# State-space loop: each projection's products in a row, conditioning columns and evictions moved, the last input matrices ahead of the state products

## The chip, the cores and the metric

One core of a Trainium2 chip runs one kernel. The metric is the device time of the whole kernel in microseconds, as the median of runs; smaller is better. The engines are TensorE (PE, with its weight loads PEld), VectorE (DVE), ScalarE (ACT), GpSimd (POOL) and SyncE (SP); the last two mostly issue transfers here. Each runs its own instructions strictly in the order in which the program has them, and waits for others by semaphores.

## The reference

Two residual layers over a sequence of 512 tokens of width 1024 in float32. The first layer mixes tokens with a state-space model (64 groups of 16 channels, 64 complex states each), the second with forgetting attention; each is followed by a gated convolutional feed-forward block, and each sub-layer is modulated by columns that a conditioning vector gives. Only the state-space layer is touched:

```python
def adaln_params(c, w, b):
    mod = jax.nn.silu(c) @ w + b
    shift, scale, gate = jnp.split(mod, 3, axis=-1)
...
def s5_mixer(h, w_in, lam_re, lam_im, log_dt, b_re, b_im, c_re, c_im, d_skip, w_glu, w_out):
    u = h @ w_in                                  # projection
    ug = u.reshape(Bsz, S, S5_GROUPS, S5_GROUP)
    ...                                           # lb: state decay, bb: input matrix
    # state[l] = lb * state[l-1] + bb @ u[l];  y[l] = Re(c @ state[l])
    y = y + d_skip.astype(f32) * u.astype(f32)
    y = jax.nn.gelu(y)
    y = y * jax.nn.sigmoid(y @ w_glu.astype(f32))
    return (y @ w_out.astype(f32)).astype(h.dtype)
```

## The kernel before

The method `s5` does this layer with channels in 8 tiles (`KT`) of 128, eight groups of channels to a tile. Time is cut in 64 blocks (`B`) of 8 steps (`L`). Inside a block the answer to the inputs is a product with a small Toeplitz matrix; from block to block the states go by a scan on VectorE. The loop over `m` in `range(KT - 2)` does tile `m`, and prepares tiles `m + 1` and `m + 2` beside it; tiles 6 and 7 follow behind the loop, in the tail. Within `tc.manual_schedule` every engine gets its instructions in the order in which the code issues them: the order of the Python lines is the order of the work, and nothing else sets it. A tile of a pool that has no free room waits until the last reader of that room is done.

The steps of iteration `m`, with the lines under which the profile has them:

- `s5_blocks(m)`, "blocks", L1089: 16 products on TensorE, block inputs into states; they need `u` and `w1` of tile m.
- `inputs(m + 1)`, "input matrices", L1029: 8 products out of `x` (a sum made by VectorE, `s5_states_in`, L991 and L1001) and of the planes `s5_both` (ScalarE, L1016). Their four results go through four PSUM rooms of the pool `aux`, which ScalarE empties into `w1` (L1034) and `kt` (L1038).
- `s5_scan(m)`: seven instructions on VectorE, L1105 to L1120, whose result is `ua`. They need the factors `cf` (ScalarE, L1074) and the rotations `rot` (made ahead on VectorE, L968 to L970, and copied on ScalarE, L977 and L983).
- `s5_kernel(m + 1)` adds to `kt` (VectorE, L1046) and stores it to DRAM (`s_z`, SP, L1049); `s5_toeplitz(m + 1)` reads it back spread out as `tw` (SP, L1056); `s5_masked(m)` makes `t` of an earlier `tw` (ScalarE, L1065, eight instructions).
- `project(m + 2)`, "projection", L1259: 8 products of 128x512, split in `steps[:4]`, `steps[4:5]`, `steps[5:6]`, `steps[6:7]` and `steps[7:]`; `done()` evicts them to `uf` (ScalarE, L1264) and stores it (`s_ud`, SP, L1265), and `read_u(m + 2)` reads it back turned (SP, L1269).
- `s5_from_inputs(m)`, "input products", L1130: 8 products of `t` and `u` into two PSUM rooms; `s5_from_states(m)`, "state products", L1141: 16 products of `ua` and `w2` (`s5_states_out`, VectorE, also L991 and L1001; two rooms) into the same two.
- `s5_gelu(m)`, "yg", L1154: two evictions on ScalarE, then a store (`s_yd`, SP, L1155); `s5_read_y` reads it back as `h` (SP, L1158).
- `next(ada)` and `next(ada2)`, "columns", L226: each call multiplies the conditioning vector with a part of the modulation matrix; two calls stand in most iterations. The last call of `ada` (in iteration 1) also evicts the sum (`ada_rows`, ScalarE, L235), and one more, in iteration 2, turns it into columns (L165, L170, L178). Their matrices are loaded by POOL (L194) into rooms that they share with the weights.
- `part_hi` (ScalarE, L1285) and `part_lo` (VectorE, L1288) split y in two parts; `head_raw` loads the first weights of `w_glu` (POOL, L194), `head_hi` and `head_lo` split them (L1295, L1299), and `glu_head` (TensorE, L1304) begins the next product in the tail.

The two arrangements of the order that matter are these: half of the projection stands ahead of the input products and the rest is scattered behind them, and yg is issued between the state products and the last projection.

Of the kernel before, what the change touches and what calls it, by code (L numbers as in the profile page):

```python
# [20 lines left out]
KT = D // P  # L21
# [58 lines left out]
class Trunk:  # L80
# [71 lines left out]
    def done(self):  # L152
        while self.bg:
            assert next(self.bg.pop(0), None) is None
# [663 lines left out]
class S5(Trunk):  # L818
# [341 lines left out]
    def s5(self, i, nxt):  # L1160
# [7 lines left out]
        with ExitStack() as stack:  # L1168
# [82 lines left out]
            us, ws, w2s, tws, cfs, kts, dds, yps = ({} for _ in range(8))  # L1251

            def run(steps):
                for f in steps:
                    f()
# [19 lines left out]
            def inputs(m, beside=None):  # L1275
                ws[m], kts[m] = self.s5_inputs(m, x_in.pop(m), beside)
# [30 lines left out]
            with tc.manual_schedule(engines={ENG.PE, ENG.Activation, ENG.DVE, ENG.SP, ENG.Pool}):  # L1307
# [35 lines left out]
                for m in range(KT - 2):  # L1343
                    if m + 3 < KT:
                        load_w(m + 3)
                    load_d(m + 2)
                    ps = self.s5_blocks(ws[m], us[m])
                    inputs(m + 1)
                    st = self.s5_scan(rot[:, :, m % 2 * 4:m % 2 * 4 + 4], ps, cfs.pop(m))
                    self.s5_kernel(m + 1, kts.pop(m + 1), dds.pop(m + 1))  # L1350
                    next(turns)
                    t = self.s5_masked(tws.pop(m))
                    tws[m + 1] = self.s5_toeplitz(m + 1)
                    if m:
                        self.s5_read_y(m - 1)
                    steps, done = project(m + 2)
                    run(steps[:4])
                    yp, outs = self.s5_from_inputs(us[m], t)
                    run(outs[:8] + steps[4:5])
                    if m == 2:  # L1360
                        next(ada)
                    run(steps[5:6] + outs[8:])
                    self.s5_planes_of(m + 2)
                    x_in[m + 2] = self.s5_states_in(m + 2)
                    if m == 2:
                        yhi = self.act.tile([P, KT, S], F32R, name="y_hi", tag="a_lo")
                        aux = self.aux.tile([KT, P], F32, name="aux")
                        nc.tensor.transpose(aux, self.sc, self.ident)
                        rows = self.tmp.tile([KT, P], F32, name="nm_h", bufs=4)
                        nc.scalar.activation(rows, aux, AF.Copy)  # L1370
                        nc.sync.dma_start(self.scd, rows)
                    if m >= 2:
                        part_hi(m - 2)
                    if m == KT - 3:
                        run(steps[6:])
                        done()
                        read_u(m + 2)
                    w2s[m + 1] = self.s5_states_out(m + 1)
                    if m % 2:
                        rot = next(turns)  # L1380
                    cfs[m + 1] = self.s5_factors(m + 1)
                    outs = self.s5_from_states(yp, w2s.pop(m), st)
                    if m < KT - 3:
                        run(outs[:16] + steps[6:7] + outs[16:])
                        self.s5_gelu(m, yp)
                        if m == 1:
                            next(ada)
                            next(ada2)
                        else:
                            next((ada, ada2)[m > 1])  # L1390
                        run(steps[7:])
                        done()
                        read_u(m + 2)
                        next((ada, ada2)[m > 1])
                    else:
                        run(outs)
                        self.s5_gelu(m, yp)
                        next(ada2)
                        inputs(KT - 1)
                        t = self.s5_masked(tws.pop(KT - 2))  # L1400
                        next(ada2)
                    us.pop(m)
                    ws.pop(m)
                    if m == KT - 4:
                        head_raw(0)
                        head_raw(1)
                    if m == KT - 3:
                        head_raw(2)
                        head_raw(3)
                    if m % 2 and m + 3 < KT:  # L1410
                        turns = self.s5_rotations(m + 3)
                        next(turns)
                m = KT - 2
                ps, ps2 = (self.s5_blocks(ws[n], us[n]) for n in (m, m + 1))
                self.s5_kernel(m + 1, kts.pop(m + 1), dds.pop(m + 1))
                self.s5_read_y(m - 1)
                tws[m + 1] = self.s5_toeplitz(m + 1)
                w2s[m + 1] = self.s5_states_out(m + 1)
                yp, outs = self.s5_from_inputs(us[m], t)
                run(outs)  # L1420
                ylo = self.act.tile([P, KT, S], F32R, name="y_lo", tag="a_hi")
                for n in range(HEAD):
                    gps[n] = self.mm.tile([P, S], F32, name="mmp")
                head_hi(0)
                part_hi(m - 2)
                head_hi(1)
                for n in range(2):
                    for k in range(5):
                        glu_head(k, 0, (n,))
# [433 lines left out]
```

## Time and profile before

| | us |
|---|---|
| median of 3 runs | 1218.91 (1216.08 to 1222.62) |
| the profiled execution | 1213.14 |
| its span in the profile | 1211.3 |
| the loop, from the input products of iteration 0 to the blocks of the tail | 64.09 to 162.38 |
| the tail, to the last state products' end | 162.38 to 180.9 |

The profile is of one execution, so its numbers add up to 1213.14 and not to the median. A row of the order of time has its start and length in us, the engine, the line, what is written and read, and how many instructions; in brackets stands idle time of the engine before it, and what ended that. A product of float32 operands is two records of TensorE. In the chain that ended last, TensorE's lines have 35% and VectorE's 5% of the span; the rest of the chain is not followed by the profile.

### The profile page before, as it was taken

The numbers are of one execution on the slowest core, as the hardware profiler recorded it, in microseconds if no ns is written. First come the engines' busy times: TensorE is split into PE (matmuls) and PEld (weight loads), VectorE is DVE, ScalarE is ACT, GpSimd is POOL, SyncE is SP. The second block draws the span as 40 slices with busy tenths as digits, with TensorE's granted clock in tenths as the row PEclk, the third lists the DMA queues.
The fourth block names the chain that finished last, engine by engine and source line by source line (L and its number), as shares of the span: only waits on it lengthen the run. The fifth ranks groups of instructions, "written<-read, shape, count | busy, mean of one in ns | idle before, by whom it ended". The sixth has DMA issues, their size and how long they took to land. (4 is left out here: it accounts for less than half of the span.)

```text
span 1211.3 us, 20642 instructions
## 1 busy us (share of the span) xinstructions
PE 1179.9 (97%) x7925; PEld 1018.7 (84%) x7925; DVE 1010.1 (83%) x1868; ACT 615.1 (51%) x1179; POOL 113.5 (9%) x194
## 2 busy tenths in 40 slices
PE   7989999999999999999999999999999999999997
PEld 2556678898889889999999788878989999999987
DVE  8968896879989999998797678876899888888865
ACT  3545553435545445555443566664366555545543
POOL 0212111100000000000000344430000000000000
PEclk9889999999999999999999999999999999999999
DMA  9658758732354555433445443432223332323331
GB/s 365 261 176 287 232 189 280 269 126 70 95 193 148 175 170 173 149 113 101 126 142 193 164 165 128 149 126 88 71 70 97 122 121 89 103 93 110 109 101 70
DMA packets 71825, 181.99 MB, mean 150 GB/s; under 512 B 23103, under 2 KB 24479, under 8 KB 70703
## 3 DMA queue, kind: packets, MB, share of 16 engines
q1 hardware_dynamic: 58767, 137.94, 34.7%
q0 software_dynamic: 11632, 41.95, 10.0%
q8 instruction: 62, 1.02, 0.3%
q10 hardware_dynamic: 1328, 0.79, 0.2%
q14 instruction: 36, 0.29, 0.1%
HBM read 173.73 MB, written 6.92 MB: 149 GB/s over the span
## 5 line engine op out<-in xcount | busy, mean ns | idle before, releaser
L301 DVE TENSOR_TENSOR w_lo<-raw,w_hi 128x1024 fp32r<-128x1024 f32 (+4 forms) x173 | 180.4, 1047 | 24.8 <-ACT w_hi L300 24.3
L300 ACT ACTIVATE w_hi<-raw 128x1024 fp32r<-128x1024 f32 (+4 forms) x173 | 153.9, 899 | 92.5 <-PE mmp L317 42.2
L317 PE MATMUL mmp<-ghi,w_lo 128*128 128x512 f32 (+1 forms) x412 | 147.6, 358 | 1.3 <-DVE w_lo L301 1.1
L317 PE MATMUL mmp<-ghi,w_hi 128*128 128x512 f32 (+1 forms) x412 | 147.8, 359 | 0.0
L317 PE MATMUL mmp<-glo,w_hi 128*128 128x512 f32 (+1 forms) x412 | 147.5, 358 | 0.0
L317 PE MATMUL mmp<-a_hi,w_hi 128*128 128x512 f32 (+1 forms) x320 | 116.7, 368 | 1.5 <-ACT a_hi L469 1.5
L586 PE MATMUL mmp<-w_hi 128*128 128x256 f32 x420 | 116.5, 277 | 1.5 <-ACT nm_h L593 1.0
L586 PE MATMUL mmp<-w_lo,w_hi 128*128 128x256 f32 x420 | 116.1, 276 | 0.0
L586 PE MATMUL mmp<-w_hi,w_lo 128*128 128x256 f32 x420 | 115.9, 277 | 0.0
L317 PE MATMUL mmp<-a_hi,w_lo 128*128 128x512 f32 (+1 forms) x320 | 114.4, 358 | 0.0
L317 PE MATMUL mmp<-a_lo,w_hi 128*128 128x512 f32 (+1 forms) x320 | 114.1, 358 | 0.0
L301 DVE TENSOR_TENSOR w_lo<-sums,w_hi 128x1024 fp32r<-128x1024 f32 x78 | 95.0, 1220 | 0.0
L593 ACT ACTIVATE nm_h<-mmp 128x256 f32<-128x256 f32 x105 | 39.4, 380 | 109.4 <-PE mmp L586 109.3
L300 ACT ACTIVATE w_hi<-sums 128x1024 fp32r<-128x1024 f32 x78 | 81.0, 1054 | 24.1 <-DVE sums L554 22.6
L317 PEld LDWEIGHTS mmp<-ghi,w_lo 128*128 128x128 f32 x412 | 77.4, 188 | 13.8 <-DVE w_lo L301 2.3
L317 PEld LDWEIGHTS mmp<-ghi,w_hi 128*128 128x128 f32 x412 | 77.4, 188 | 10.4
L317 PEld LDWEIGHTS mmp<-glo,w_hi 128*128 128x128 f32 x412 | 77.4, 188 | 10.3
L586 PEld LDWEIGHTS mmp<-w_hi 128*128 128x128 f32 x420 | 78.9, 188 | 2.3 <-ACT nm_h L593 1.3
L399 DVE SCALAR_TENSOR_TENSOR h<-mmp,par,h 128x512 f32<-128x512 f32 (+1 forms) x104 | 68.8, 665 | 12.6 <-PE mmp L317 12.5
L586 PEld LDWEIGHTS mmp<-w_lo,w_hi 128*128 128x128 f32 x420 | 78.9, 188 | 0.0
L586 PEld LDWEIGHTS mmp<-w_hi,w_lo 128*128 128x128 f32 x420 | 78.7, 188 | 0.0
L586 PE MATMUL mmp<-a_hi,w_lo 128*128 128x256 f32 x280 | 77.7, 277 | 0.8 <-DVE w_lo L301 0.8
(333 smaller groups left out, 3136.1 us busy)
## 6 DMA issues: line engine op xcount, KB each, us to landing
raw<-in_w_up SPq DMA_DIRECT2D x88, 512.0 KB, 3.7
ada_raw<-in_ada_t POOLq DMA_DIRECT2D x40, 512.0 KB, 4.0
raw<-in_ada_w POOLq DMA_DIRECT2D x24, 512.0 KB, 6.5
nf<-nfd SPq DMA_DIRECT2D x8, 1152.0 KB, 7.1
raw<-in_ada_w SPq DMA_DIRECT2D x16, 512.0 KB, 7.9
raw<-in_fox_qk SPq DMA_DIRECT2D x16, 512.0 KB, 3.6
raw<-in_w_down SPq DMA_DIRECT2D x24, 320.0 KB, 3.0
rawd<-in_w_down SPq DMA_DIRECT2D x24, 256.0 KB, 3.1
```

Source lines behind the costliest of these rows:

```text
L300: self.rounded = nc.scalar.activation(hi, src, AF.Copy).ins
L301: return nc.vector.tensor_tensor(lo, src, hi.bitcast(F32), ALU.subtract)
L317: self.last_mm = self.nc.tensor.matmul(o if len(xt.shape) == 2 else by_place(o), wt, xt, start=(k == 0 and n == 0), stop=(k == nk - 1 and ...
L399: add = self.nc.vector.scalar_tensor_tensor(h, ps, self.par[i][:, 16 + m:17 + m], h, op0=ALU.mult, op1=ALU.add,)
L586: self.last_mm = nc.tensor.matmul(o, wt[:, k], xt[:, k], start=(first and k == 0 and n == 0), stop=(k == H - 1 and n == 2), skip_group_che ...
L593: a = nc.scalar.activation(t, o, AF.Copy)
```

## The change

The projection's products are issued in a row, ahead of the input products, in every iteration; in iteration 2 the gate's columns are turned between its two halves. Its eviction and `read_u` follow at once. The input products and the state products come behind them side by side, and then both calls of `next(ada)` or `next(ada2)`. The eviction yg of iteration `m` is now issued in iteration `m + 1`, behind its blocks, instead of ahead of the last projection. In iteration 5 (`KT - 3`) the last input matrices, their `t` and the sum into `kt` come ahead of the state products, and yg behind these. In the tail the last columns come behind the blocks of both tiles, and two loads and three ScalarE splits are issued elsewhere. Nothing is computed that was not computed before.

TensorE from iteration 0 to the start of iteration 1, before (-) and now (+); `ua` and `w_576` are the operands of the state products, `s_sc` is the conditioning vector:

```order
 L1029 MATMUL aux<-s_both_138,x 128x2x80 x8
-L1259 MATMUL mmp<-a_x,raw 128x512 x4
+L1259 MATMUL mmp<-a_x,raw 128x512 x8
 L1130 MATMUL aux<-u,t 128x64 x8
-L1259 MATMUL mmp<-a_x,raw 128x512 x2
 L1141 MATMUL aux<-ua,w_576 128x63 x16
-L1259 MATMUL mmp<-a_x,raw 128x512
-L226 MATMUL mmp<-raw,s_sc_206 32x512 x4
-L1259 MATMUL mmp<-a_x,raw 128x512
-L226 MATMUL mmp<-raw,s_sc_206 32x512 x4
+L226 MATMUL mmp<-raw,s_sc_206 32x512 x8
 L1089 MATMUL aux<-u,w_647 64x64 x16
```

The four projection products that stood behind the input products have moved ahead of them, and the two groups of columns stand together; iterations 1, 3 and 4 change in the same way.

ScalarE at the end of iteration 1 and the start of iteration 2 (`w_954` is the `w1` that the input matrices of iteration 2 fill):

```order
 L1016 ACTIVATE s_both_138<-s_rr 64x2x64 x2
+L235 ACTIVATE ada_rows<-mmp 128x512
 L983 ACTIVATE rot<-rot 128x512
 L1074 ACTIVATE cf<-s_mask,s_mag_181 128x2x64 x4
+L977 ACTIVATE rot<-s_rot 128x16x8
 L1154 ACTIVATE yg<-aux 128x256 x2
-L1264 ACTIVATE uf<-mmp 128x512
-L235 ACTIVATE ada_rows<-mmp 128x512
-L977 ACTIVATE rot<-s_rot 128x16x8
 L1034 ACTIVATE w_954<-aux 128x2x128
```

The eviction of the columns' sum now stands ahead of the rotations, the factors and yg, and yg directly ahead of the next matrices.

TensorE from iteration 5 into the tail:

```order
 L1130 MATMUL aux<-u,t 128x64 x8
-L1259 MATMUL mmp<-a_x,raw 128x512 x4
-L1141 MATMUL aux<-ua,w_1354 128x63 x16
-L226 MATMUL mmp<-raw,s_sc_206 32x512 x4
 L1029 MATMUL aux<-s_both_138,x 128x2x80 x8
+L1141 MATMUL aux<-ua,w_1351 128x63 x16
 L226 MATMUL mmp<-raw,s_sc_206 32x512 x4
 L1089 MATMUL aux<-u,w_1430 64x64 x16
-L1089 MATMUL aux<-u,w_1548 64x64 x16
+L1089 MATMUL aux<-u,w_1524 64x64 x16
+L226 MATMUL mmp<-raw,s_sc_206 32x512 x4
 L1130 MATMUL aux<-u,t 128x64 x8
```

The last input matrices have moved ahead of the state products and the columns, and the last group of columns behind the blocks.

The diff:

```diff
@@ -1345,6 +1345,8 @@
                         load_w(m + 3)
                     load_d(m + 2)
                     ps = self.s5_blocks(ws[m], us[m])
+                    if m:
+                        self.s5_gelu(m - 1, yps.pop(m - 1))
                     inputs(m + 1)
                     st = self.s5_scan(rot[:, :, m % 2 * 4:m % 2 * 4 + 4], ps, cfs.pop(m))
                     self.s5_kernel(m + 1, kts.pop(m + 1), dds.pop(m + 1))
@@ -1355,12 +1357,12 @@
                         self.s5_read_y(m - 1)
                     steps, done = project(m + 2)
                     run(steps[:4])
-                    yp, outs = self.s5_from_inputs(us[m], t)
-                    run(outs[:8] + steps[4:5])
                     if m == 2:
                         next(ada)
-                    run(steps[5:6] + outs[8:])
+                    run(steps[4:])
+                    done()
                     self.s5_planes_of(m + 2)
+                    read_u(m + 2)
                     x_in[m + 2] = self.s5_states_in(m + 2)
                     if m == 2:
                         yhi = self.act.tile([P, KT, S], F32R, name="y_hi", tag="a_lo")
@@ -1371,59 +1373,54 @@
                         nc.sync.dma_start(self.scd, rows)
                     if m >= 2:
                         part_hi(m - 2)
-                    if m == KT - 3:
-                        run(steps[6:])
-                        done()
-                        read_u(m + 2)
                     w2s[m + 1] = self.s5_states_out(m + 1)
+                    yp, outs = self.s5_from_inputs(us[m], t)
+                    run(outs)
+                    outs = self.s5_from_states(yp, w2s.pop(m), st)
+                    if m < KT - 3:
+                        run(outs)
+                        yps[m] = yp
+                        if m == 1:
+                            next(ada)
+                            next(ada2)
+                            next(ada)
+                        else:
+                            next((ada, ada2)[m > 1])
+                            next((ada, ada2)[m > 1])
                     if m % 2:
                         rot = next(turns)
                     cfs[m + 1] = self.s5_factors(m + 1)
-                    outs = self.s5_from_states(yp, w2s.pop(m), st)
-                    if m < KT - 3:
-                        run(outs[:16] + steps[6:7] + outs[16:])
-                        self.s5_gelu(m, yp)
-                        if m == 1:
-                            next(ada)
-                            next(ada2)
-                        else:
-                            next((ada, ada2)[m > 1])
-                        run(steps[7:])
-                        done()
-                        read_u(m + 2)
-                        next((ada, ada2)[m > 1])
-                    else:
+                    if m == KT - 3:
+                        inputs(KT - 1)
+                        t = self.s5_masked(tws.pop(KT - 2))
+                        self.s5_kernel(KT - 1, kts.pop(KT - 1), dds.pop(KT - 1))
                         run(outs)
                         self.s5_gelu(m, yp)
-                        next(ada2)
-                        inputs(KT - 1)
-                        t = self.s5_masked(tws.pop(KT - 2))
                         next(ada2)
                     us.pop(m)
                     ws.pop(m)
                     if m == KT - 4:
                         head_raw(0)
                         head_raw(1)
-                    if m == KT - 3:
-                        head_raw(2)
-                        head_raw(3)
                     if m % 2 and m + 3 < KT:
                         turns = self.s5_rotations(m + 3)
                         next(turns)
                 m = KT - 2
                 ps, ps2 = (self.s5_blocks(ws[n], us[n]) for n in (m, m + 1))
-                self.s5_kernel(m + 1, kts.pop(m + 1), dds.pop(m + 1))
+                head_raw(2)
+                head_hi(0)
+                part_hi(m - 2)
+                head_hi(1)
+                next(ada2)
+                head_raw(3)
+                tws[m + 1] = self.s5_toeplitz(m + 1)
                 self.s5_read_y(m - 1)
-                tws[m + 1] = self.s5_toeplitz(m + 1)
                 w2s[m + 1] = self.s5_states_out(m + 1)
                 yp, outs = self.s5_from_inputs(us[m], t)
                 run(outs)
                 ylo = self.act.tile([P, KT, S], F32R, name="y_lo", tag="a_hi")
                 for n in range(HEAD):
                     gps[n] = self.mm.tile([P, S], F32, name="mmp")
-                head_hi(0)
-                part_hi(m - 2)
-                head_hi(1)
                 for n in range(2):
                     for k in range(5):
                         glu_head(k, 0, (n,))
```

## The prediction

> **What bounds the kernel now.** I read the page's busy shares first, then a table of stretches over the state-space loop, then who waited for whom in it, then the order of time on each engine.
>
> ```profile
> PE 1179.9 (97%) x7925; PEld 1018.7 (84%) x7925; DVE 1010.1 (83%) x1868; ACT 615.1 (51%) x1179; POOL 113.5 (9%) x194
> ```
> ```profile
> 60.00:64.00 4.00, 0.00 (x0) 0.00 (x0) 3.90 (x7) 2.53 (x9) 0.00 (x0) 0.99 0.22 60
> 64.00:71.00 7.00, 6.91 (x20) 4.59 (x20) 4.72 (x4) 3.01 (x8) 0.00 (x0) 0.52 0.32 100
> 77.06:93.49 16.43, 16.43 (x133) 9.95 (x129) 14.28 (x17) 7.90 (x26) 2.60 (x6) 1.00 0.83 291
> 143.98:162.38 18.40, 18.40 (x148) 12.31 (x144) 14.63 (x19) 10.69 (x37) 2.01 (x4) 1.00 0.65 210
> 162.00:168.00 6.00, 6.00 (x96) 5.19 (x89) 5.87 (x8) 5.25 (x12) 0.53 (x1) 1.00 0.89 322
> 173.00:176.00 3.00, 3.00 (x13) 2.45 (x12) 2.83 (x5) 2.77 (x10) 0.00 (x0) 0.53 0.07 20
> ```
> ```profile
> ACT yg L1154 <- PE aux L1141: 6.0, 1, 6.0
> ...
> PE aux L1130 <- ACT t L1065: 4.2, 1, 4.2
> ```
>
> In the stretches the columns are PE, weight loads, DVE, ACT, POOL, then the granted clock; in the waits, the total, how often, the longest. TensorE sets the pace: in iteration 1 (77.06 to 93.49) and iteration 5 (143.98 to 162.38) it is busy throughout, while VectorE has 14.28 of 16.43 and 14.63 of 18.40 us. So the same products in another order gain only where TensorE stands still or runs slowly. In the loop it stands still twice: 4.2 us in iteration 0, for t of ScalarE, and 2.3 us in the tail (row of 171.15 below). Behind each the clock falls to half (0.52 and 0.53).
>
> **Iteration 0.** TensorE, in order of time:
>
> ```profile
> 56.30 3.60 PE L1259 MATMUL mmp<-a_x,raw 128*128 128x512 f32 x8
> 64.09 3.68 PE L1130 MATMUL aux<-u,t 128*128 128x64 f32 x16 [4.19 <-ACT t L1065]
> 67.56 3.54 PE L1259 MATMUL mmp<-a_x,raw 128*128 128x512 f32 x4
> 71.03 2.00 PE L1141 MATMUL aux<-ua,w 64*128 64x63 f32 x32
> ...
> 77.06 1.15 PE L1089 MATMUL aux<-u,w 128*64 128x64 f32 x32
> ```
> ScalarE, SP's queue, the landings of u in this time, VectorE:
>
> ```profile
> 61.47 2.57 ACT L1065 ACTIVATE t<-tw,first 128x128 f32<-128x128 f32 x8 [4.46 <-DMA tw<-s_z]
> ```
> ```profile
> 62.18 0.37 SPq L1269 DMA_DIRECT2D u<-s_ud  x1
> ```
> ```profile
> DMA to landing us min/median/max: 2.8/2.9/3.0
> ```
> ```profile
> 67.56 1.22 DVE L1001 TENSOR_TENSOR w<-w,x 128x1024 f32<-128x1024 f32 x1
> ```
>
> Each projection product is two records; starts, not modelled ends, give the pace. Four of eight run from 56.30, TensorE then stands 4.19 us until the masked kernel t is out of ScalarE, and the other four come behind it. The change puts all eight ahead. A full-clock product takes 0.86 us (96.85 to 100.28 for four, below), so the eight end at 63.2 and 0.9 us of the gap is left. t comes as before: nothing ahead of it moves. Behind 64.09 stand only the input products (1.73, 83.86 to 85.59 below), the state products (87.45 to 89.38, 1.93) and eight column products (two groups of 1.00, some 1.95 together): 5.6 us instead of 12.97. The next blocks start at 69.7 instead of 77.06: **-7.4 us**, if the clock stays whole. What they need is there: u was issued at 62.18 and lands within 3.0, by 65.2; VectorE is done at 68.8. On ScalarE uf (0.6, as ada_rows of the same size below) moves ahead of planes, factors, table load and yg. Before, these were done 6.0 us ahead of the state products' end (first wait above: 73.0, so at 67.0); with uf, 67.6, and the state products now end at 67.8. So yg starts as soon as it can. uf's own two transfers on SP also come sooner, which only helps: they are wanted an iteration later.
>
> The price I cannot read is the clock. With 0.9 us left, and with input and state products now side by side (3.66 us of short products), it could fall as before. If it is half until 70.8, as the stretch shows (0.52 over 64 to 71 is half for some 6.7 us), 3.35 of the 5.6 us of work is done by then and 2.25 remain: blocks at 73.0, a gain of 4.0. I take -7.4, since the nearest stretch of short products without a gap, 162 to 168 (blocks and input products), ran at 1.00. Bounds -4.0 and -7.4.
>
> The Trainium skill (TensorE: Matmul & The Clock Gate, Part 1) has the clock halve only after a whole idle window of about 3.4 us. The trace differs: the gap of 2.34 us in the tail was enough. By the page the term is -7.4; by the tail's row alone 0.9 us is merely below the shortest gap seen to hurt.
>
> **Iterations 1, 3 and 4.** The steady order, with the products that are joined:
>
> ```profile
> 83.86 1.89 PE L1130 MATMUL aux<-u,t 128*128 128x64 f32 x16
> 85.59 1.94 PE L1259 MATMUL mmp<-a_x,raw 128*128 128x512 f32 x4
> 87.45 2.00 PE L1141 MATMUL aux<-ua,w 64*128 64x63 f32 x32
> 89.38 1.13 PE L1259 MATMUL mmp<-a_x,raw 128*128 128x512 f32 x2
> 90.44 1.07 PE L226 MATMUL mmp<-raw,s_sc 128*32 128x512 f32 x8
> 91.44 1.13 PE L1259 MATMUL mmp<-a_x,raw 128*128 128x512 f32 x2
> 92.49 1.07 PE L226 MATMUL mmp<-raw,s_sc 128*32 128x512 f32 x8
> 96.85 3.60 PE L1259 MATMUL mmp<-a_x,raw 128*128 128x512 f32 x8
> 100.28 1.89 PE L1130 MATMUL aux<-u,t 128*128 128x64 f32 x16
> ```
>
> The last four projections take 1.86 + 1.06 + 1.05 = 3.97 us scattered and 3.43 in a row: 0.54 less, and 0.1 from joined columns. I take **-0.65 each, -1.95**; bounds 0 and -0.65, as TensorE can only keep what VectorE's 2.1 us of slack allows. No wait comes back by this order's starts: state products begin 12.0 us into an iteration instead of 10.4, and VectorE's scan is done at 6.5 (1.1 of blocks, 5.4 of its own by the tail's rows); the eviction yg stays ahead of the next inputs. Column tiles and weights are loaded an iteration ahead from POOL, whose order is unchanged; some rooms come free sooner. On SP the yd store now stands behind the projection's two transfers; its reader comes an iteration later, at no cost.
>
> **Iteration 2.** On ScalarE the rows of the first gate columns now stand ahead of rot, factors, rot and yg of iteration 1, all of which used to be done before.
>
> ```profile
> 86.42 1.26 ACT L1074 ACTIVATE cf<-s_mask,s_mag 128x128 f32<-128x128 f32 x4
> 89.53 0.66 ACT L1154 ACTIVATE yg<-aux 128x256 f32<-128x256 f32 x2 [1.85 <-issue]
> 93.65 0.60 ACT L235 ACTIVATE ada_rows<-mmp 128x512 f32<-128x512 f32 x1 [0.41 <-PE mmp L226]
> 94.14 0.30 ACT L977 ACTIVATE rot<-s_rot 128x128 f32<-128x128 f32 x1
> ```
>
> With the larger rot copy (128x512, taken as ada_rows' 0.60) that is 3.4 us behind the last column product. The third input product, which needs yg's room, would start 1.1 (blocks) and two products of 0.57 behind it (93.49 to 96.85 hold blocks and inputs, 3.36), so 2.25. A wait of 1.0 (0 if the copies are hidden, 1.2 by the whole difference), less the 0.65: **+0.35**; bounds -0.65 and +0.55. Behind it ScalarE's t has 6 us to spare.
>
> **Iteration 5 and the tail.**
>
> ```profile
> 156.09 2.00 PE L1141 MATMUL aux<-ua,w 64*128 64x63 f32 x32
> 162.38 2.08 PE L1089 MATMUL aux<-u,w 128*64 128x64 f32 x64
> 171.15 2.00 PE L1141 MATMUL aux<-ua,w 64*128 64x63 f32 x32 [2.34 <-DVE ua L1120]
> 173.08 2.43 PE L1304 MATMUL mmp<-y_hi,w_hi 128*128 128x512 f32 x5
> 175.31 2.51 PE L1130 MATMUL aux<-u,t 128*128 128x64 f32 x16
> 177.63 1.42 PE L1304 MATMUL mmp<-y_hi,w_hi 128*128 128x512 f32 x5
> ```
> ```profile
> 155.02 1.23 DVE L1001 TENSOR_TENSOR x<-x,x 128x1024 f32<-128x1024 f32 x1
> 162.24 1.22 DVE L991 TENSOR_TENSOR w<-s_pr,s_rr 128x1024 f32<-128x1024 f32 x1
> 165.77 0.68 DVE L1105 TENSOR_TENSOR m<-aux,rot 128x512 f32<-128x512 f32 x1
> ```
>
> From the iteration's start (143.98) the last input matrices now come at 12.2, when VectorE's x is ready (155.02 + 1.23), with only two of four PSUM rooms, so the third product waits until ScalarE, held by uf, planes, y_hi, rot and factors until about 13.7, has emptied the first. They end at 15.4, the state products at 17.35 instead of 14.0. VectorE's next w waits for these (it takes their room), then takes 3.5 us (162.24 to 165.77), the scan 5.4 (165.77 to 171.15): next state products at 26.35 instead of 27.17, **-0.8**. TensorE's own work ahead of them ends at 25.5, so its gap shrinks from 2.34 to 0.85. Then the half clock of 173 to 176 may go: it costs now 1.0 in five products (2.43 against 1.42 in the last row) and 0.6 in the input products (2.51 against 1.89). I take **-1.2** of these 1.6, the rest being left for ScalarE's last t, which those input products also need. Bounds of the tail: +1.5 (gap as before, and another such fall of the clock behind the new wait) to -2.8 (2.3 of gap less 0.9 left of it, and 1.6, less 0.2 for what the wait adds).
>
> On the queues: SP puts the last matrix's z ahead of the yd store, and tw ahead of the read of y, each a few us earlier than it is wanted. POOL keeps its order, but the third w_glu load waits for the room of column products that now come at 18.4 instead of 15.0; ScalarE wants it behind the factors that follow the scan, at some 25. I take no cost for 6 us of lead; if late, it is in the +1.5.
>
> **Sum.** -7.4 - 1.95 + 0.35 - 2.0 = -11.0 us. The profiled execution took 1213.14 us (span 1211.3); it becomes 1202.1. The runs' median is 1218.91, 5.8 above it; the same step gives **1208 us**. Behind the tail TensorE is again without a pause, so I expect the step to be kept.
>
> **Rivals.**
> 1. *The clock falls in iteration 0 all the same*: -4.0 in place of -7.4, and the tail keeps its own fall (-0.8 for -2.0): -6.4 us, 1212.5. For it, the short products side by side; against it, 162 to 168. Chance 0.2.
> 2. *The tail turns into a new wait*: two PSUM rooms, and w behind the state products: +1.5 for -2.0, so -7.5 us, 1211.4. For it, the late 17.35; against it, VectorE's chain still ends 0.8 earlier by the steps above. Chance 0.12.
> 3. *The gap only moves*: t comes, but the next blocks wait for something of old (a load under a busy queue), -2 to -4 us, 1216. Against it, u's landing at 65.2. Chance 0.07.
> 4. *Slower*: half clock in every iteration, since a window can now fall inside 3.66 us of short products. Each such fall costs 1.7 us (half of 3.4); seven undo the 11.0, two in each of six iterations cost 20, so +9 and 1228. It decides at about one fall an iteration. Against it, the 1.00 of 162 to 168. Chance 0.05.
> Forecast: 0.56.
>
> **Numbers.** About 0.5% (6.1 us) can be told from no change here. Forecast and rival 2 are faster, rival 1 stands on the line (a quarter of it faster), rival 3 is the same: faster 0.74, same 0.21, slower 0.05. The range goes from -16 (every lower bound, -13, and the 3 us that runs of one kernel spread) to -3.5 (rival 1 with that spread): 1203 to 1215.4; without rivals 1205 to 1211.
>
> **What would show it.** The wait of L1130 for t falls below 1.5 us and the clock of the stretch behind it reads 1.00; projections stand eight in a row, iterations 1, 3, 4 take 15.8 us; the third input product of iteration 2 waits about 1 us for yg; L1141 waits 0.9 us in the tail. Wrong if the stretch behind t stays at 0.5, if the loop's iterations grow beyond 16.4, or if TensorE first waits later in the kernel for the 11 us that it came early.

## The result and the profile after

The changed kernel takes 1210.41 us (median of 10 runs, 1203.20 to 1213.52), the kernel before 1217.85 us (10 runs, 1214.96 to 1222.62). The medians are 7.4 us apart; the ratio of the runs is 0.9931, with a 95% interval of 0.9909 to 0.9954, which is 8.4 us less, between 5.6 and 11.1. It is faster, by less than the 11.0 us of the sum. In the comparisons further down, two slow runs of the kernel before (1662 and 1678 us, at a granted clock near 0.66) are left out of every figure. The execution that was profiled took 1211.51 us (span 1209.7), only 1.6 less than the profiled one of before, with the loop's mechanism half as forecast and half not.

TensorE is still busy for 97% of the span:

```profile
PE 1178.8 (97%) x7925; PEld 1021.4 (84%) x7925; DVE 1009.6 (83%) x1868; ACT 615.0 (51%) x1179; POOL 113.4 (9%) x194
```

Iteration 0 and the two behind it, TensorE in order of time, and ScalarE's t (start, length, line, what; idle time before it in brackets):

```profile
56.21 7.03 PE L1259 MATMUL mmp<-a_x,raw 128*128 128x512 f32 x16
65.42 2.85 PE L1130 MATMUL aux<-u,t 128*128 128x64 f32 x16 [2.18 <-ACT t L1065]
68.20 3.68 PE L1141 MATMUL aux<-ua,w 64*128 64x63 f32 x32
71.81 3.64 PE L226 MATMUL mmp<-raw,s_sc 128*32 128x512 f32 x16
75.38 1.69 PE L1089 MATMUL aux<-u,w 128*64 128x64 f32 x32
...
91.75 1.15 PE L1089 MATMUL aux<-u,w 128*64 128x64 f32 x32
...
94.39 1.87 PE L1029 MATMUL aux<-s_both,x 128*128 128x160 f32 x12 [0.74 <-DVE m L1106]
...
109.80 1.15 PE L1089 MATMUL aux<-u,w 128*64 128x64 f32 x32
...
125.63 1.15 PE L1089 MATMUL aux<-u,w 128*64 128x64 f32 x32
```
```profile
62.81 2.56 ACT L1065 ACTIVATE t<-tw,first 128x128 f32<-128x128 f32 x8 [5.89 <-DMA tw<-s_z]
```

The stretches around it (columns as in the prediction; the clock stands third from the end):

```profile
63.00:66.40 3.40, 1.22 (x10) 0.98 (x9) 3.37 (x4) 3.36 (x12) 0.00 (x0) 0.99 0.40 96
66.40:76.60 10.20, 10.20 (x80) 6.99 (x80) 2.26 (x2) 3.15 (x7) 2.56 (x5) 0.50 0.57 157
109.80:125.63 15.83, 15.83 (x132) 10.37 (x128) 14.29 (x17) 8.71 (x28) 3.72 (x8) 1.00 0.89 294
```

The eight projections stand in a row and end at 63.2, as forecast. But t starts at 62.81 instead of 61.47, so 2.18 us of the gap are left instead of 0.9. Behind it the clock is half from 66.4 to 76.6, which is three windows of 3.41 us; before it was two. So the blocks of iteration 1 start at 75.38 instead of 77.06: 1.7 us gained here, not 7.4. Iteration 3 takes 15.83 us, as forecast (15.8); iteration 2 (91.75 to 109.80) 18.05, 0.40 more than before (row below), with a wait of 0.74 us at the third input product.

```profile
93.49:111.14 17.65, 17.65 (x144) 11.15 (x140) 14.27 (x20) 9.09 (x30) 4.10 (x8) 1.00 0.82 271
```

The tail:

```profile
168.10 2.00 PE L1141 MATMUL aux<-ua,w 64*128 64x63 f32 x32 [0.68 <-DVE ua L1120]
...
173.59 1.41 PE L1304 MATMUL mmp<-y_hi,w_hi 128*128 128x512 f32 x5
174.93 2.00 PE L1141 MATMUL aux<-ua,w 64*128 64x63 f32 x32
```

The wait for ua is 0.68 instead of 2.34, and the five products behind it take 1.41 instead of 2.43: the half clock of the tail is gone in this execution.

### The profile page after: what moved, and what is told of

Same layout as the page of the kernel before. It is cut to its first block, busy times and chain, and to the rows that moved or that the text cites. A ratio compares the mean times of both kernels' runs of the same rounds, so it can differ in the third digit from the quotient of the medians.

```text
span 1209.7 us, 20643 instructions
## 1 busy us (share of the span) xinstructions
PE 1178.8 (97%) x7925; PEld 1021.4 (84%) x7925; DVE 1009.6 (83%) x1868; ACT 615.0 (51%) x1179; POOL 113.4 (9%) x194
## 4 chain that ended last, share of the span: by engine, by line
PE 59%; issue 20%; DVE 11%; DMA 5%; ACT 2%; POOL 1%; SPq 0%; DVEq 0%; POOLq 0%; ACTq 0%
PE mmp L317 26%; PE mmp L586 13%; PE aux L586 5%; PE mmp L1259 2%; DVE w_lo L301 2%; PE aux L1719 1%; PE mmp L1580 1%; PE aux L1739 1%; PE mmp L226 1%; PE aux L1141 1%; DMA rawd<-in_w_down 1%; PE aux L1029 1%; POOL ada_raw L256 1%; PE mmp L1196 1%; PE aux L1689 1%
```

## Experiments: which part brings how much

All runs of one comparison were made beside runs of the kernel before; the three comparisons are of three chips, so a row is compared with the kernel before of its own table. "Clock loss" below is a run's time multiplied by one minus its mean granted clock; "at whole clock" is the rest. They were used because a median alone mixes two things that the change moves. The clock loss is an upper bound of what half clock cost: each of the 13 profiled executions is also at half clock for its last 3.3 to 6.5 us, behind TensorE's last product. And it is not all the loop's: each has a fall near 40 us, and five have one window at half clock between 409 and 437 us, far behind the loop.

**The kernel before again.** No edit.

> The kernel before, once more, so that each of its runs has its granted clock beside its time. Theory: a run's time is set by how many windows of 3.41 us the clock stays at half, each costing 1.7 us. Its profiled run had five such windows in the loop and a mean clock of 0.991; the median of its runs lies 4 to 5 us above that run, so they should show 0.986 to 0.989 (two to three windows more), and time and clock should fall on one line of some 12 us per 0.01. Rival: the runs differ for another reason (transfers); then slow and quick runs show the same clock, 0.991.

Measured: 1216.18 us (median of 11 runs), ratio 0.9997 (0.9979 to 1.0014). Its runs show clocks from 0.988 to 0.993, and time goes with them (correlation 0.78, 1.3 us of time for each us of clock loss; 0.70 and 0.9 over all 79 runs of the kernel before on the three chips). The theory holds in kind: the clock goes with a good part of the spread, not with all of it. The clocks were a little higher than expected (mean 0.9904). Its profiled execution shows what varies:

```profile
62.70 2.75 PE L1130 MATMUL aux<-u,t 128*128 128x64 f32 x16 [2.57 <-ACT t L1065]
65.23 2.90 PE L1259 MATMUL mmp<-a_x,raw 128*128 128x512 f32 x4
```
```profile
63.80:67.10 3.30, 3.30 (x11) 2.27 (x11) 3.27 (x4) 1.85 (x3) 0.00 (x0) 0.50 0.39 93
67.20:74.10 6.90, 6.90 (x56) 2.88 (x54) 1.77 (x2) 1.25 (x3) 1.69 (x4) 1.00 0.37 101
```

The same program waited 2.57 us for t here, against 4.19 in the profile that the prediction read, and the half clock lasted one window, not two. So the gap of iteration 0 differs from one execution to the next.

**Iteration 0 alone.** The kernel before, with the order of `m == 0` taken from the changed kernel (its yg goes into iteration 1; the diff is cut at "..."):

```diff
                     run(steps[:4])
+                    if m == 0:
+                        run(steps[4:])
+                        done()
...
+                    if m == 0:
+                        yp, outs = self.s5_from_inputs(us[0], t)
+                        run(outs)
+                        run(self.s5_from_states(yp, w2s.pop(0), st))
+                        next(ada)
+                        next(ada)
```

> The kernel before with the new order in iteration 0 alone (its projection in one piece, input and state products and columns side by side behind it). Theory: the order saves the gap of t in part, but the clock falls behind it all the same for one to three windows, so 1.7 to 5 us here, 3.4 in the middle (1214.4 against 1217.8), and the wait of L1130 for t stays near 2 us. Rival as predicted: 7.4 us, 1210.4, clock whole behind t. Rival, nothing: the gain sits in the later iterations and the tail, 1217.8.

**The rest alone.** The changed kernel, with `m == 0` in the order of before (four projections, input products among two more, state products).

> The changed kernel with iteration 0 in the old order (four projections, input products, two projections, state products). Theory: iterations 1, 3 and 4 save 0.6 each, iteration 2 costs 0.4, iteration 5 and the tail save 2.6 with the half clock of the tail gone: 4.0 us, 1213.8. The stretch of half clock behind t is as before (two windows). Rival: all of the gain is iteration 0's: 1217.8. Rival: iteration 0 gives nothing: 1209.4.

**Iteration 5 and the tail alone.** The kernel before, with `m == KT - 3` and the tail of the changed kernel.

> The kernel before with iteration 5 and the tail alone as in the changed kernel (last input matrices and t ahead of the state products, column products behind the last blocks). Theory: from the start of iteration 5 to the end of the last state products 36.9 us become 35.4, and with what the products behind gain from the whole clock 2.6 us in all: 1215.2; no half clock between 150 and 190 us. Rival: the tail's half clock was left out for a reason that lies in earlier iterations (the phase of the windows): it falls again here, and the gain is 0.8, 1217.

Measured, ratios to before and means of the runs:

| | runs | ratio (interval) | mean us | clock loss | at whole clock |
|---|---|---|---|---|---|
| before, beside these | 34 | | 1217.87 | 11.61 | 1206.26 |
| iteration 0 alone | 12 | 0.9958 (0.9938 to 0.9978) | 1212.67 | 10.01 | 1202.66 |
| the rest alone | 12 | 0.9974 (0.9960 to 0.9989) | 1213.15 | 9.10 | 1204.04 |
| iteration 5 and tail alone | 12 | 0.9982 (0.9970 to 0.9994) | 1215.12 | 9.42 | 1205.70 |
| changed kernel, first time (beside other runs of before) | 10 | 0.9931 (0.9909 to 0.9954) | 1209.57 | 7.63 | 1201.94 |

The two halves multiply to 0.9932, the whole change is 0.9931. Neither "all of it is iteration 0" nor "iteration 0 gives nothing" is left. Iteration 0 brings about 5 us, which lies between the theory's 3.4 and the predicted 7.4; the tail 2 to 3 (by its interval 0.7 to 3.7); iterations 1 to 4 the difference between the rest alone and the tail alone, about 2.

In the profiled execution of iteration 0 alone, t left early enough:

```profile
64.06 2.00 PE L1130 MATMUL aux<-u,t 128*128 128x64 f32 x16 [1.12 <-ACT t L1065]
...
69.77 1.15 PE L1089 MATMUL aux<-u,w 128*64 128x64 f32 x32
```
```profile
64.00:69.77 5.77, 5.71 (x64) 4.14 (x64) 4.02 (x4) 4.15 (x11) 0.49 (x1) 1.00 0.61 165
```

The gap is 1.12, the clock stays at 1.00 although input and state products stand side by side, and the next blocks start at 69.77, where the prediction had 69.7. So in these profiles the order does what was forecast when the gap is near one microsecond, and does not when it is two. Iteration 0 in the old order (the rest alone) and the tail in the new one:

```profile
63.59 3.68 PE L1130 MATMUL aux<-u,t 128*128 128x64 f32 x16 [4.46 <-ACT t L1065]
```
```profile
170.76 2.00 PE L1141 MATMUL aux<-ua,w 64*128 64x63 f32 x32 [0.68 <-DVE ua L1120]
```
```profile
160.00:181.00 21.00, 19.99 (x235) 15.96 (x233) 18.96 (x26) 13.80 (x36) 3.14 (x6) 1.00 0.71 217
```

The first row is of the rest alone, the others of the tail alone: its wait is 0.68 and its stretch at 1.00, though iteration 0's clock fell in that execution as before. None of the eight profiled executions with the new tail has a fall between 150 and 190 us. But the old tail does not always have one. In iteration 0 alone, whose tail is that of before, TensorE waits 2.33 us for ua, as it did before, and the clock stays whole:

```profile
163.85 2.00 PE L1141 MATMUL aux<-ua,w 64*128 64x63 f32 x32 [2.33 <-DVE ua L1120]
```
```profile
159.91:163.33 3.42, 1.61 (x8) 0.98 (x6) 3.32 (x5) 1.54 (x6) 0.00 (x0) 1.00 0.59 207
163.33:166.74 3.41, 2.89 (x36) 2.69 (x37) 3.17 (x5) 3.41 (x9) 0.00 (x0) 1.00 0.00 0
```

The other four profiles with the old tail have a fall there. So the rival, that what earlier iterations shift decides whether the tail's clock falls, holds in part: one and the same gap made it fall or not. What the new tail brings is a shorter wait (0.68 us here), behind which no profile shows a fall.

## Experiments: what makes the clock fall, and for how long

**Short products behind the gap.** The kernel before, iteration 0 only:

```diff
-                    run(outs[:8] + steps[4:5])
-                    run(steps[5:6] + outs[8:])
+                    run(outs)
...
-                        run(outs[:16] + steps[6:7] + outs[16:])
+                        run(outs + steps[4:7])
```

> The kernel before; in iteration 0 the four projection products that stood among the input and state products now stand behind them all, so that the gap of 4 us stays and only short products (64 columns) follow it. Theory (a fall lasts until a window of 3.41 us holds mostly 512-column products): input and state products take 3.7 + 3.9 us at half clock, the fall lasts three to four windows (10.2 to 13.7 us) instead of two (6.8), and the time grows by 1.7 to 3.4 us to 1219.5 to 1221, mean clock 0.001 to 0.003 lower. Rival (a fall lasts as long as the gap set, whatever follows): two windows, 1217.8 as before.

Measured: 1221.71 us against 1215.50, ratio 1.0044 (1.0029 to 1.0058). At whole clock it takes 1205.57, the kernel before beside it 1205.49; the clock loss is 16.0 against 10.7. By this reckoning all of the slowdown is the clock's.

```profile
64.45 3.67 PE L1130 MATMUL aux<-u,t 128*128 128x64 f32 x16 [5.72 <-ACT t L1065]
68.05 3.68 PE L1141 MATMUL aux<-ua,w 64*128 64x63 f32 x32
71.66 4.29 PE L1259 MATMUL mmp<-a_x,raw 128*128 128x512 f32 x6
```
```profile
61.00:74.60 13.60, 10.15 (x52) 8.37 (x53) 6.21 (x6) 6.20 (x17) 0.00 (x0) 0.50 0.30 85
173.60:183.80 10.20, 10.20 (x52) 8.94 (x50) 9.99 (x15) 4.03 (x12) 1.34 (x3) 0.50 0.37 82
```

The fall lasts four windows, the first of them still in the gap. TensorE works from 64.45 on without a pause, but only the window with the 512-column products of 71.66 ends it. (The tail's fall took three windows in this execution, also with input and state products in it; so the 5.3 us of additional clock loss are not all iteration 0's.) That explains the three windows in the changed kernel's profile: behind its gap stand 64-column products alone until 71.81. Putting them side by side does not make the clock fall (iteration 0 alone, 64.06 to 67.92, at 1.00), but once it has fallen it keeps it down. The 13 profiles agree: between 55 and 185 us, the windows that ended a fall held 1.9 to 3.2 us of 512-column products, and those behind which the fall went on 0 to 1.4 us.

The Trainium skill (TensorE: Matmul & The Clock Gate, Part 1) has a free-running window of about 3.4 us, half clock after an idle window and whole clock after a busy one. The trace agrees on the window (in all 13 profiles every fall in the loop and the tail lasts a multiple of 3.41 us) and differs on both conditions: the changed kernel's clock fell after a window with 2.18 idle of 3.41 us, and in the stretch above two windows (64.38 to 71.20, with TensorE at work from 64.45 on) left it at half.

**The store sooner.** The changed kernel; the first matrix's kernel no longer waits for VectorE's last level of rotation tables (three instructions, about 2.0 us; the expectation speaks of two levels):

```diff
                 next(turns)
-                next(turns)
                 self.s5_kernel(0, kts.pop(0), dds.pop(0))
+                next(turns)
                 rot = next(turns)
```

> The changed kernel with the first matrix's kernel (the sum into kt and its store to s_z) ahead of the last two levels of VectorE's rotation tables, 2.4 us sooner. Theory (idle gap): t then leaves ScalarE some 2.4 us sooner, at 60 to 61 instead of 62.8 for its first piece, the projection's eight products end at 62.9, and of the gap of 1.1 to 2.2 us in front of L1130 at most 0.5 is left; the clock stays whole through iteration 0. On the mean this saves about 1.6 us of gap and the 1.6 us of half clock that iteration 0 alone still showed: 3.2 us less than the changed kernel (1210.4), so about 1207 and a mean clock of 0.995. Rival (short products): the clock falls because 3.7 us of 64-column products stand side by side; then it falls here too, the mean clock stays at 0.9935 and the time at 1209. Rival (transfers): tw's landing is set by the loads around it, not by the store, and t comes as late as before: 1210.4.

**The columns first.** The changed kernel, in iteration 0 with both `next(ada)` ahead of the input products, in the gap.

> The changed kernel with the two groups of column products of iteration 0 (1.9 us) ahead of the input products, in the gap for t, instead of behind the state products. Theory (idle gap): the gap of 1.1 to 2.2 us becomes 0 to 0.4, the next blocks start 1.1 to 1.9 us sooner, and the clock stays whole: 1.5 + 1.6 = 3.1 us less than the changed kernel, about 1207.3, mean clock 0.995. Rival (short products): input and state products still stand side by side, with the blocks behind them (4.8 us of 64-column products), so the clock falls as often or more often: 1209, clock 0.993.

**Both waits.** The store sooner, and in iteration 1 (the two added lines are skipped further down for `m == 1`):

```diff
                         if m == 1:
+                            rot = next(turns)
+                            cfs[2] = self.s5_factors(2)
                             next(ada)
```

> As the kernel with the first matrix's store sooner, and in iteration 1 the rotation copy and the factors on ScalarE ahead of the copies of the column products. Theory: the wait of 0.7 us of iteration 2 (L1029 for m of L1106, which waits for the rotation copy) goes, iteration 2 takes 17.4 instead of 18.05 us: 0.6 us less than that kernel, about 1206.4. Rival: the column products' rooms then come free later and the wait turns to them: iteration 2 stays at 18 us.

Measured:

| | runs | median us | ratio (interval) | clock loss | at whole clock |
|---|---|---|---|---|---|
| before, beside these | 15 | 1215.50 | | 10.70 | 1205.49 |
| store sooner | 6 | 1204.96 | 0.9899 (0.9877 to 0.9921) | 5.62 | 1198.95 |
| columns first | 6 | 1205.41 | 0.9911 (0.9891 to 0.9930) | 5.43 | 1200.27 |
| both waits | 5 | 1203.40 | 0.9893 (0.9872 to 0.9913) | 5.05 | 1198.46 |

The store sooner: SP's issues of the store and of its reader, ScalarE's t, TensorE's wait for it:

```profile
47.59 0.32 SPq L1049 DMA_DIRECT2D s_z<-kt  x1
52.45 0.32 SPq L1056 DMA_DIRECT2D tw<-s_z  x1
```
```profile
60.48 2.57 ACT L1065 ACTIVATE t<-tw,first 128x128 f32<-128x128 f32 x8 [4.37 <-DMA tw<-s_z]
```
```profile
63.10 2.00 PE L1130 MATMUL aux<-u,t 128*128 128x64 f32 x16 [0.66 <-ACT t L1065]
```

Columns first, and both waits:

```profile
63.40 1.92 PE L226 MATMUL mmp<-raw,s_sc 128*32 128x512 f32 x16
65.26 2.00 PE L1130 MATMUL aux<-u,t 128*128 128x64 f32 x16
```
```profile
83.58 1.15 PE L1089 MATMUL aux<-u,w 128*64 128x64 f32 x32
84.66 2.44 PE L1029 MATMUL aux<-s_both,x 128*128 128x160 f32 x16
...
100.64 1.15 PE L1089 MATMUL aux<-u,w 128*64 128x64 f32 x32
```

Two edits that have nothing in common but the gap, one that shortens the wait and one that fills it, bring the clock loss 5.1 and 5.3 us below that of the kernel before beside them; for the changed kernel the distance is 4.0 in the table above and 3.6 in the one below. All 17 runs of this table with an edit have a mean clock of 0.994 or more, but only 8 of the changed kernel's 18. With the columns first, input products, state products and blocks stand in a row (65.26 to 70.20, 4.9 us of products of 63 and 64 columns) and the clock loss is the second lowest of the table: the rival that short products alone bring the clock down falls. The rival that the loads set tw's landing is not settled by the row of 60.48: with the store in its old place t starts anywhere from 60.08 to 62.81 in nine profiles. But in the three other profiles with the store sooner it starts at 56.30 to 56.62, ahead of all of those; with both waits:

```profile
56.62 2.57 ACT L1065 ACTIVATE t<-tw,first 128x128 f32<-128x128 f32 x8 [0.65 <-DMA tw<-s_z]
```

So the store counts, and the landing of its transfers still spreads t. With both waits, iteration 2 takes 17.06 us (83.58 to 100.64) and its input products no longer wait, as they still do with the store sooner alone (0.74 us); the 1.0 us that this saves against 18.05 shows in the profile, but the times of the two kernels are not told apart.

**All three edits; the store sooner on the kernel before; the changed kernel again.**

> The changed kernel with all three edits: first store sooner, column products of iteration 0 ahead of its input products, rotation copy and factors of iteration 1 ahead of the copies of the column products. Theory: with the store sooner the gap for t is 0 to 0.7 us already, so the columns in it add 0.3 us on the mean over the kernel with the store and the rotation copy alone: ratio to before 0.989, mean clock 0.996, iteration 0 without a wait of TensorE for t in its profile. Rival: the columns ahead take PSUM rooms or ScalarE's time from what the next blocks need, and it is slower than that kernel: 0.991.

> The kernel before with the first matrix's store sooner alone, order of products as before. Theory: the gap of L1130 for t goes from 4.3 to about 1.9 us (2.4 us saved), and the half clock behind it now falls in a part of the executions, since what decides is how much of one window of 3.41 us is idle (0.35 of a window did nothing, 0.64 made it fall): 1.7 us more saved on the mean, 4.1 in all, ratio 0.9966, mean clock 0.992. Rival: any gap near 2 us makes it fall as the tail's 2.3 does, and the four dense products behind end it after one window: ratio 0.9975. Rival: the gap follows the loads, not the store: 1.000.

> The changed kernel once more, on the chip of its best version. Theory: ratio 0.993 as before, mean clock 0.9935, time at whole clock (each run's time less what its clock lost) 4 to 6 us below before's: the parts alone gave 3.6 (iteration 0) and 2.2 (the rest). Rival: a part of the parts' gain is given back later when both are in (the two profiles showed 2.6 us of it between 360 and 650 us): then 4 us or less again at whole clock.

| | runs | median us | ratio (interval) | clock loss | at whole clock |
|---|---|---|---|---|---|
| before, beside these | 19 | 1216.67 | | 11.60 | 1205.60 |
| all three edits | 6 | 1203.54 | 0.9886 (0.9866 to 0.9905) | 5.22 | 1198.23 |
| store sooner on before | 12 | 1210.41 | 0.9946 (0.9923 to 0.9969) | 8.28 | 1202.41 |
| changed kernel again | 8 | 1209.16 | 0.9932 (0.9906 to 0.9957) | 8.02 | 1201.02 |

All three edits make the best kernel, 1.1% below the kernel before, though not to be told from both waits or from the store sooner alone. The store sooner on the kernel before brings 0.9946; the 0.9966 expected lies at the end of its interval. One line moved on VectorE brings about what the new order of iteration 0 brought (0.9958). In its profiled execution there is no gap in iteration 0 at all, where 1.9 us were expected, but the tail's fall came all the same (its wait for ua is 0.96, since TensorE had already waited 1.20 us for u at the blocks before it):

```profile
59.18 1.89 PE L1130 MATMUL aux<-u,t 128*128 128x64 f32 x16
...
162.89 2.00 PE L1141 MATMUL aux<-ua,w 64*128 64x63 f32 x32 [0.96 <-DVE ua L1120]
```
```profile
161.96:165.37 3.41, 2.48 (x34) 2.35 (x35) 3.13 (x6) 3.41 (x8) 0.00 (x0) 1.00 0.04 17
165.40:172.10 6.70, 6.70 (x25) 5.55 (x23) 6.63 (x11) 2.11 (x7) 1.31 (x3) 0.50 0.53 125
```

The changed kernel's second profiled execution took 1203.37 us, and is the case that the forecast described:

```profile
63.93 2.00 PE L1130 MATMUL aux<-u,t 128*128 128x64 f32 x16 [0.82 <-ACT t L1065]
...
69.64 1.15 PE L1089 MATMUL aux<-u,w 128*64 128x64 f32 x32
...
168.63 2.00 PE L1141 MATMUL aux<-ua,w 64*128 64x63 f32 x32
```
```profile
64.00:69.64 5.64, 5.64 (x64) 4.07 (x64) 4.21 (x4) 4.02 (x10) 0.49 (x1) 1.00 0.62 165
```

The last state products, which ended at 180.91 before, end at 170.56 here (1.93 behind the last start), 10.35 us sooner, and the span is 1201.6 against 1211.3, 9.7 less: nearly all of it is kept to the end. In the first profile 4.05 us were gained at this place and 1.6 at the end; that loss does not come back in the second, so the change does not bring it in every execution; where it comes from is open. By the whole-clock column the change saves 4.6 us here and 4.3 in the first table, at the lower end of the theory's 4 to 6.

## Why the prediction was right, and where it was not

It said 1208 us and 1203 to 1215.4; the median is 1210.41. By its own steps, in us of mean time (the parts are differences of the rows above, each with a standard error of 0.5 to 0.8 us; the clock's are of the whole run, wherever in it the clock was lost):

| step | forecast | measured |
|---|---|---|
| iteration 0, gap and joined products, at whole clock | -4.0 | -3.6 |
| iteration 0, half clock avoided | -3.4 | -1.6 |
| iterations 1 to 4 at whole clock (-1.95 + 0.35) | -1.6 | -1.66 |
| iteration 5 and tail, VectorE's chain | -0.8 | -0.56 |
| iteration 5 and tail, half clock avoided | -1.2 | -2.2 |
| sum | -11.0 | -9.9 by the parts with 0.3 of clock in iterations 1 to 4, -8.3 whole |

- *Iteration 0* is the term that was mis-sized: "-7.4 us, if the clock stays whole" (in the table split in two windows of half clock, 3.4, and the other 4.0). The step that failed was to take "0.9 us of the gap is left" from one execution as the gap of all. The profiles show 0.82, 1.12 and 2.18 us in the new order (2.57 to 5.72 in the old one), since t comes behind two transfers whose landing varies. With 0.82 and 1.12 the clock stayed whole and the blocks started at 69.64 and 69.77, for 69.7 forecast. With 2.18 it fell, for longer than before. For iteration 0 the forecast and rival 1 were both right, each for a part of the executions. How large a part can be estimated: all six profiles without a fall between 55 and 185 us have a mean clock of 0.994 or more, the seven with one 0.993 or less. By that mark 8 of the changed kernel's 18 runs had no such fall (mean 1206.1 us) and 10 had one (1212.0). The median within the range is the mix of the two, so its place is in part luck; the reason for which rival 1 expected the fall, the short products side by side, was not the cause, and its other half, the tail's fall, came in no profile with the new tail.
- *The side-by-side short products*: the prediction set them beside the stretch of 162 to 168 and rightly found no fall of their own. What it missed is that they lengthen one that something else has started.
- *Iterations 1, 3, 4* took 15.83 or 15.84 us instead of 16.42 (iteration 1 in the second profile; in the first it took 16.37, 1.2 of it at half clock), a saving of 0.59 where 0.65 was forecast. *Iteration 2*: +0.40 for +0.35. The wait came at the place named, with 0.74 us for 1.0, but not for yg's room, as the step had it: the product starts at 94.39, ahead of yg.

```profile
94.44 0.63 ACT L1154 ACTIVATE yg<-aux 128x256 f32<-128x256 f32 x2
```

The profile puts the wait down to VectorE's m (L1106), which ends at 94.24. With both waits the input products run through while L1106 ends at 86.07, behind the third product's start (about 85.2), so it is hardly that either. That the edit to ScalarE's order removed the wait shows that this order is the cause; which of its instructions TensorE waited for stays open.
- *The tail*: the wait for ua is 0.68 (0.85 forecast). Counted from the start of iteration 5 (141.47), the state products end at 17.57 (17.35 forecast) and the next ones start at 26.63 (26.35 forecast, 27.17 before), so VectorE's chain saved 0.54 and not 0.8; the terms given, 17.35 + 3.53 + 5.38, add up to 26.26. What waits for a room there is the fifth product of the input matrices, the first one of the third result. From the start of iteration 5 to the end of the last state products 36.9 us became 35.4, so 1.5 of the forecast 2.0 in these two profiles; over the runs it seems more, and the tail's fall does cost more than one window in some executions (three in the row of 173.60, whose tail is that of before) and none in others (iteration 0 alone). Rival 2 (a new wait in the tail) did not come, nor rival 3 or 4.
- Whether the parts' 9.9 and the change's 8.3 differ is open: the two are 1.6 apart, and each has a standard error of more than 1. The parts need not add up either: iteration 0 alone lost its tail's fall in the profile, as the tail alone did, so both may count the same fall.

## What to carry to other kernels

A gap that waits for a transfer has a spread: before a forecast leans on what is left of it, look at several executions, or say what the term is at both ends of it. Judge a stall on TensorE by the stretch behind it as well as by its length, and put wide products directly behind it: in the loop and the tail a fall of the clock ended only in windows with 1.9 us or more of 512-column products, and two windows of it cost 3.4 us, nearly as much as the stall of 4.19. And look first for what makes the awaited thing late; here one addition standing behind one level of tables on VectorE was worth about as much as a new order of iteration 0's products on TensorE.

## What the runs showed of the hardware

- Idle time alone does not decide a fall. In iteration 0 alone the gap of 1.12 us, in a window whose rest was mostly the projection's 512-column products, did nothing, and neither did the tail's window of 159.91 to 163.33 with 1.81 us idle, all its products being of 512 columns. In the store sooner on before, the window of 161.96 to 165.37 had 0.93 us idle and 1.93 us of 64-row state products, and the clock fell. What is counted (columns, rows, work at half clock as half) no run here tells.
- Each of the 13 profiled executions has a fall near 40 us that no long wait explains. In the kernel with both waits, TensorE was busy for 2.67 of 3.40 us, but mostly with products of one and two columns. The fall ended behind one window of the input matrices' 160-column products alone, so 512 columns are not needed to end one:

```profile
38.43 1.95 PE L1242 MATMUL aux<-par,raw 128*128 128x1 f32 x16 [0.27 <-ACT par L178]
40.84 4.08 PE L1029 MATMUL aux<-s_both,x 128*128 128x160 f32 x16 [0.46 <-issue]
```
```profile
37.50:40.90 3.40, 2.67 (x23) 2.53 (x23) 3.23 (x9) 2.60 (x6) 0.95 (x2) 1.00 0.55 193
40.95:44.30 3.35, 3.35 (x13) 3.35 (x14) 3.32 (x6) 2.79 (x8) 0.00 (x0) 0.50 0.20 78
```

- A store to DRAM and the landing that SP waits for before it issues the reader took 4.9 us in the row of 47.59 and 5.6 in the profile of the kernel before (49.52 to 55.16), but 1.6 in the kernel before run again (49.78 to 51.34). The reader's own transfer of tw spreads as much, from 3.0 to 8.7 us from issue to landing, and partly makes up for it: in the kernel before run again it took 8.7 instead of 6.3, so t came only 1.4 us sooner (60.08 for 61.47). Both transfers spread t; what spreads them is open.
